# Two-layer encoder on one core: operand sums of the output product made one by one, additions to the rows by accumulating transfers, the last gate's addition two groups behind its product

## The chip, the core and the metric

The kernel runs on one core of a Trainium2 chip. The metric is device time in microseconds. The core's engines work in parallel, each through its own list of instructions in order: TensorE (PE, matrix products; PEld are its weight loads), VectorE (DVE), ScalarE (ACT), GpSimd (POOL) and SyncE (SP, which only issues transfers here). They wait for one another through semaphores. A transfer (DMA) is issued from the list of SP, ACT or POOL and then runs on its own; a transfer that adds to what stands at its target is issued from POOL here.

## What is computed

The model has two layers over 512 tokens of width 1024, with 256 memory tokens. Layer 0 mixes by dilated window attention, layer 1 by grouped-query attention; both also attend to the memory. Everything is in 32-bit floats.

```python
def reference(x, mem, norm_g, mem_norm_g, w_mem_kv, mem_qn_g, mem_kn_g, w_out, w_in_a, qn_a, kn_a, w_in_b, qn_b, kn_b):
    ...
    for i in range(DEPTH):
        h = rmsnorm(x, norm_g[i])
        mem_h = rmsnorm(mem, mem_norm_g[i])
        ...
            proj = jnp.einsum('bsd,de->bse', h, w_in_a[j])
            ...
            gate = proj[..., n_qkv + MEM_W:]
            o_mix = mixer_dilated(qkv, qn_a[j], kn_a[j], ang_a)
        ...
        o_mem = memory_attention(q_mem, mem_h, w_mem_kv[i], mem_qn_g[i], mem_kn_g[i])
        y = jnp.concatenate([o_mix, o_mem], axis=-1) * jax.nn.silu(gate)
        x = x + jnp.einsum('bse,ed->bsd', y, w_out[i])
    return x
```

The change touches the last two lines of the loop in both layers: the gated `y` (512 tokens by 1536), its product with `w_out`, and the addition to `x`.

## The kernel before

**A product in three matmuls.** Each operand is split into a high part of reduced precision and a low part with the rest. `mm3` (lines 162 to 165) multiplies high by high, high by low and low by high. Weights arrive as 128x1024 tiles `wl`; ACT casts the high part `wh` (line 285), DVE subtracts it for the low part `wo` (line 295). Of a tile of `y` the same pair is made by `put` (line 762 on ACT, 763 on DVE).

**Seven products for eight.** `s_chunk` multiplies a 2x2 grid of blocks with seven block products instead of eight, out of sums of blocks (Winograd's form). The products are called 12, 11, S1, S2, S4, S3 and 22, after the sums that go in. Each goes into a bank of PSUM (`pj`, four banks in rotation; a product marked fresh takes a new one, another adds to the bank of an earlier one). When a bank is complete, `keep` copies it to a tile `sn` (ACT, line 360) or `add` adds it to such a tile (DVE, line 370), which gives a block of the result that goes to `ev`; a `keep` also makes one difference (DVE, line 364). Until that copy or addition has read the bank, the product that takes the bank next can't start.

**The order is written out.** The program is traced once and each engine runs its instructions in the order of the trace. A `Driver` counts groups of matmuls ("slots"): `s_chunk` calls `tick` after each weight tile, and work that has been handed over with `release` (drains of banks, with a delay in slots), `spawn` (urgent) or `later` (bulk) is traced when its slot comes. A `yield n` in such work means: go on n slots later. So where an instruction stands in DVE's or ACT's list is decided by these delays.

**The output projection.** `gates` makes the gated `y` in three chunks of 512 columns: m (the memory heads), a and b (the mixer's two halves). Chunks m and a are held as `yf`, and `prep_y` (lines 751 to 795) makes from them the left operands of the seven products: 12 and 11 as they are; then, in `ys` and in place, S1 = a21 - a22, S2 = S1 - a11, S4 = a12 + S2 and S3 = a11 - a21, and last 22. Chunk b's blocks (tanh, lines 725 to 743) make `y` for a plain product in `out_rest`. `out_proj` (lines 797 to 815) loads the rows that are added to (`acc`, line 804: x, or layer 0's result), runs the seven products with 512-column tiles, whose `ev` adds each block `t` to `acc` (line 812, DVE), and then `out_rest` (line 696), which adds the product of chunk b and gives each block of rows on: to the norm of the next layer, or to the output.

In time the pieces overlap. Chunk b of the gates is still being drained when the products 12 and 11 run. In layer 0 the last head's softmax scaling (`p`, line 1097), its transposition (`pt`, line 1110) and its product also fall into the seven products, and behind them the norm of the memory rows of layer 1 (POOL, lines 412, 413 and 453). In layer 1 the attention heads run all through them, four blocks of 128 queries for each head: scores, `nmb` (the row maximum, line 1314), exponentials, `rdb` and `pb` (lines 1323, 1324), a transposition on PE, and `pbT`, whose high part ACT casts (line 1337) and whose low part DVE subtracts (line 1342), before PE multiplies by the values into `ob`.

Names in the profile: `sn` is a drained block, `th` a tanh, `og` the attention's output read back from memory (`od`, `odb`), `yS` a sum's pair of parts, `y` either the pair of 12, 11 and 22 or that of chunk b.

Of the kernel before, what the change touches and what calls it, by code (L numbers as in the profile page):

```python
# [13 lines left out]
ALU = mybir.AluOpType  # L14
# [110 lines left out]
def trunk_kernel(ctx: ExitStack, tc: tile.TileContext, x, mem, wall, norm_g, mem_norm_g, gcol,  # L125
                 qn_a, kn_a, qn_b, kn_b, ident_d, mask_d, tab_a, tab_b, out):
    nc = tc.nc
    V, A, G, T = nc.vector, nc.scalar, nc.gpsimd, nc.tensor
# [14 lines left out]
    def s2(dt=F32, name="s2"):  # L143
        return pool.tile([128, 512], dt, tag="s2", name=name, bufs=NS2)
# [204 lines left out]

    PRODUCTS = (("12", 0, True), ("11", 1, True), ("S1", 0, True), ("S2", 1, False), ("S4", 0, False), ("S3", 1, False), ("22", 0, True))  # L350

    def s_chunk(n, act, ev, tokens=True, pre=None, half=False):


        units, per = n // 256, 1024 // n
        bank, snap = [None, None], {}

        def keep(name, u, b):
            t = snap[name, u] = s2(name="sn")
            A.copy(t, b)  # L360
            yield 1
            if name == "s3":
                c = snap["s5", u]
                V.tensor_tensor(c, c, t, ALU.subtract)  # L364
                yield 1
                yield from ev("22", u, c)

        def add(q, name, u, b):
            t = snap[name, u]
            V.tensor_tensor(t, b, t, ALU.subtract if q == "12" else ALU.add)  # L370
            yield 1
            yield from ev(q, u, t)

        after = ((keep, "z"), (add, "11", "z"), (keep, "s5"), (keep, "s2"), (add, "12", "s2"), (keep, "s3"), (add, "21", "s3"))
        for i, (a, s, fresh) in enumerate(PRODUCTS):
            while a not in act:
                drv.tick()
            if fresh:
                bank[s] = [pj() for _ in range(units)]
            for x in range(units):  # L380
                wh, wo = [t.rearrange("p (k c) -> p k c", c=n) for t in W.take()]
                ah, al = act[a][:, 0], act[a][:, 1]
                for b in range(2):
                    if pre and i == x == 0 and b:
                        pre()
                    if half and b:
                        n_half[0] += 1
                        if n_half[0] % half == 0:
                            drv.half()
                    o = bank[s][b] if units == 2 else bank[s][0][:, b * 256:(b + 1) * 256]  # L390
                    bs = slice(b * 128, (b + 1) * 128)
                    for k in range(per):
                        kk = x * per + k
                        st, sp = fresh and kk == 0 and (units == 2 or b == 0), kk == 3
                        if tokens:
                            mm3(o, ah[:, kk, bs], al[:, kk, bs], wh[:, k], wo[:, k], st, sp)
                        else:
                            mm3(o, wh[:, k, bs], wo[:, k, bs], ah[:, kk], al[:, kk], st, sp)
                drv.free()
                W.advance()  # L400
                if x == units - 1:
                    f, *arg = after[i]
                    for u in range(units):
                        d = 2 if f is keep else 2 + u + (units == 1 and i == 6)
                        drv.release(f(*arg, u, bank[s][u]), d)
                drv.tick()

# [15 lines left out]
    half = pool.tile([128, 8], F32, name="half")  # L423
# [280 lines left out]
    def gates(od, o_done):  # L704

        ys, yf, y_done, YW = [None] * 4, [None, None], set(), {}

        def gate(H, first, g, half=False):


            yt = [[m4(F32R, "y").rearrange("p (h t) -> p h t", h=2) for _ in range(2)] for _ in range(2)] if g == 2 else None
            if g < 2:
                yf[g] = [m4(name="yf") for _ in range(2)]

            def ev(q, u, t):
# [12 lines left out]
                yield 1  # L728
                if not o:
                    while not {h0, h0 + 1} <= o_done:  # L730
                        yield 1
                    o = load()
                    yield 1
                if g < 2:
                    V.tensor_tensor(yf[g][j][:, i * 512:(i + 1) * 512], t, o, ALU.mult)
                    y_done.add((g, i, j))
                    return
                V.tensor_tensor(t, t, o, ALU.mult)
                yield 1
                tv = t.rearrange("p (h t) -> p h t", h=2)  # L740
                A.copy(yt[j][0][:, :, ts], tv)
                yield 1
                V.tensor_tensor(yt[j][1][:, :, ts], tv, yt[j][0][:, :, ts].bitcast(F32), ALU.subtract)
                y_done.add((g, i, j))
                if {(2, 0, j), (2, 1, j)} <= y_done:
                    for k in range(2):
                        ys[2 * j + k] = (yt[j][0][:, k], yt[j][1][:, k])

            s_chunk(256, H, ev, tokens=False, half=half)

        def prep_y():

            def wait(*gi):
                while not {(g, i, j) for g, i in gi for j in range(2)} <= y_done:
                    yield 1

            def put(k, src):
                t = big(F32R, "y" + k)
                for j in range(2):
                    js = slice(j * 512, (j + 1) * 512)  # L760
                    lo = t[:, 1024 + j * 512:1024 + (j + 1) * 512]
                    A.copy(t[:, js], src[j])
                    V.tensor_tensor(lo, src[j], t[:, js].bitcast(F32), ALU.subtract)  # L763
# [12 lines left out]
            s1 = [s2(name="ys") for _ in range(2)]  # L776
            s2_ = [s2(name="ys") for _ in range(2)]
            for j in range(2):
                V.tensor_tensor(s1[j], a21[j], a22[j], ALU.subtract)
            for j in range(2):  # L780
                V.tensor_tensor(s2_[j], s1[j], a11[j], ALU.subtract)
            yield 1
            put("S1", s1)
            yield 1
            put("S2", s2_)
            for j in range(2):
                V.tensor_tensor(a12[j], a12[j], s2_[j], ALU.add)
            for j in range(2):
                V.tensor_tensor(a21[j], a11[j], a21[j], ALU.subtract)
            yield 1  # L790
            for k, src in (("S4", a12), ("S3", a21), ("22", a22)):
                put(k, src)
                yield 1

        return gate, prep_y, YW, ys

    def out_proj(YW, ys, src, evac, tiles, half=False):

        acc, done = {}, set()

        def load():
            for i in range(2):
                for u, t in enumerate(tiles()):
                    nc.sync.dma_start(t, src[2 * i + u])
                    acc[2 * i + u] = halves(t)
                yield 2

        def ev(q, u, t):
            b, n = 2 * (int(q[0]) - 1) + u, int(q[1]) - 1
            while b not in acc:  # L810
                yield 1
            V.tensor_tensor(acc[b][n], t, acc[b][n], ALU.add)
# [26 lines left out]
    H, H2 = {}, {}  # L839
# [321 lines left out]
    gate, prep_y, YW, ys = gates(od, o_done)  # L1161
# [217 lines left out]
    gate, prep_y, YW, ys = gates(od_b, o_done_b)  # L1379
# [121 lines left out]
```

## Time and profile before

| | us |
|---|---|
| median of 3 runs | 982.19 (982.18 to 983.54) |
| the profiled execution, whole | 981.91 |
| its span, first to last instruction | 980.1 |
| DVE adding to `acc` at line 812, 16 times | 683 ns each |
| DVE idle, 580 to 600 and 900 to 920 | 1.19 and 0.11 |
| DVE idle, 600 to 620 and 920 to 940 | 3.53 and 1.99 |

The page lists each engine's busy time and share of the span. A row of PE's waits says which PE instruction waited for which instruction of another engine, for how long in total, how often, and the longest. A row of a timeline has the start, the duration, the engine, the line, the operation and the tiles (out <- in), and in brackets how long the engine sat idle ahead of it and what ended that. On DVE durations overlap a little with the next start, so the cost of an operation in a row of them is the distance of two starts. A row of the windows gives the length, then busy time (and count) of PE, PEld, DVE, ACT and POOL, the clock granted to TensorE, the share of the DMA engines and GB/s. The output projection of layer 0 lies at about 575 to 650 us, that of layer 1 at about 910 to 980.

### The profile page before, as it was taken

What the parts mean: (1) busy time and instruction counts of PE and PEld (TensorE: products, weight loads), DVE (VectorE), ACT (ScalarE), POOL (GpSimd) and SP (SyncE); (2) the same over time, 40 slices, a digit from 0 to 9 for tenths busy, and PEclk for the clock granted to TensorE, in tenths of its full rate; (3) what the DMA queues carried; (4) which work ended last, traced back from release to release, by engine and by line L of the source; (5) the groups of instructions that cost most, each with busy time, mean ns of one, the idle gap of its engine ahead of it and who ended that gap; (6) DMA issues with size and microseconds to landing.
All of it is one profiled execution on the core that took longest, in us unless ns stands there. A gap on an engine that the chain in (4) does not pass through costs nothing.

```text
span 980.1 us, 16658 instructions
## 1 busy us (share of the span) xinstructions
PE 953.1 (97%) x5728; PEld 839.5 (86%) x5728; DVE 825.1 (84%) x1489; ACT 645.7 (66%) x1623; POOL 332.2 (34%) x468
## 2 busy tenths in 40 slices
PE   8899999999999999999999989998999999998998
PEld 5789888888888888888899977887999999997786
DVE  6997788878888888888888998968789998889974
ACT  5556678686767676768676656455677766667650
POOL 1121424556555555555544010124533331011000
PEclk9999999999999999999999999999999999999999
DMA  8979846969686868686949795669695786786432
GB/s 328 329 267 322 227 97 183 290 129 266 152 253 154 251 157 248 158 249 136 271 124 295 228 251 158 258 224 329 168 209 140 189 220 165 230 207 148 144 129 86
DMA packets 86678, 205.08 MB, mean 209 GB/s; under 512 B 25025, under 2 KB 35777, under 8 KB 86594
## 3 DMA queue, kind: packets, MB, share of 16 engines
q1 hardware_dynamic: 70034, 146.28, 42.7%
q0 software_dynamic: 15264, 55.58, 30.1%
q10 hardware_dynamic: 1296, 2.16, 0.6%
q8 instruction: 45, 0.74, 0.3%
q14 instruction: 39, 0.32, 0.1%
HBM read 157.79 MB, written 12.65 MB: 174 GB/s over the span
## 4 chain that ended last, share of the span: by engine, by line
PE 75%; DVE 16%; DMA 3%; issue 2%; ACT 2%; POOL 1%; SPq 0%; DVEq 0%; POOLq 0%
PE pj L163 20%; PE pj L165 19%; PE pj L164 19%; DVE wo L295 4%; PE qT L534 2%; PE oo L1131 1%; PE sa L1029 1%; PE pt L1110 1%; PE sa L1025 1%; PE xT L464 1%; DMA od<-o 1%; DVE sn L370 1%; PE ptb L1333 1%; DVE nmb L1314 1%; DVE yS L763 1%
## 5 line engine op out<-in xcount | busy, mean ns | idle before, releaser
L295 DVE TENSOR_TENSOR wo<-wl,wh 128x1024 fp32r<-128x1024 f32 x255 | 315.5, 1242 | 8.4 <-ACT wh L285 8.0
L285 ACT CAST wh<-wl 128x1024 fp32r<-128x1024 f32 x255 | 269.9, 1059 | 74.1 <-PE pj L165 39.8
L163 PE MATMUL pj<-wh,hS 128*128 128x512 f32 (+1 forms) x448 | 164.3, 367 | 0.2 <-ACT sn L360 0.2
L164 PE MATMUL pj<-wo,hS 128*128 128x512 f32 (+1 forms) x448 | 158.1, 353 | 2.6 <-DVE wo L295 2.6
L165 PE MATMUL pj<-wh,hS 128*128 128x512 f32 (+1 forms) x448 | 158.1, 353 | 0.0
L163 PE MATMUL pj<-wh,h 128*128 128x512 f32 (+1 forms) x336 | 123.2, 367 | 0.0
L164 PE MATMUL pj<-wo,h 128*128 128x512 f32 (+1 forms) x336 | 118.8, 353 | 1.9 <-DVE wo L295 1.9
L165 PE MATMUL pj<-wh,h 128*128 128x512 f32 (+1 forms) x336 | 118.9, 354 | 0.0
L413 POOL TENSOR_TENSOR rstd<-mse,half 128x4 f32<-128x4 f32 (+2 forms) x98 | 103.4, 1055 | 8.2
L164 PEld LDWEIGHTS pj<-wo,hS 128*128 128x128 f32 x448 | 85.0, 190 | 13.4 <-DVE wo L295 3.5
L165 PEld LDWEIGHTS pj<-wh,hS 128*128 128x128 f32 x448 | 84.7, 189 | 12.4 <-DVE hS L160 0.3
L163 PEld LDWEIGHTS pj<-wh,hS 128*128 128x128 f32 x448 | 84.8, 189 | 10.3 <-ACT sn L360 0.4
L360 ACT COPY sn<-pj 128x512 f32<-128x512 f32 x132 | 73.6, 591 | 17.5 <-PE pj L165 17.1
L412 POOL TENSOR_SCALAR mse<-hss 128x4 f32<-128x4 f32 (+1 forms) x86 | 45.7, 532 | 110.2 <-ACT junk L522 103.2
L522 ACT ACTIVATE junk<-sn 128x128 f32<-128x128 f32 x264 | 79.0, 308 | 0.2 <-DVE sn L364 0.2
L973 POOL TENSOR_TENSOR ta<-sn,tabs 128x128 f32<-128x128 f32 (+1 forms) x64 | 37.0, 580 | 120.7 <-DVE sn L527 81.6
L164 PEld LDWEIGHTS pj<-wo,h 128*128 128x128 f32 x336 | 64.0, 191 | 9.5 <-DVE wo L295 2.2
L165 PEld LDWEIGHTS pj<-wh,h 128*128 128x128 f32 x336 | 63.7, 190 | 9.2 <-DVE h L160 0.2
L370 DVE TENSOR_TENSOR sn<-pj,sn 128x512 f32<-128x512 f32 x99 | 67.5, 683 | 4.6 <-PE pj L165 4.4
L163 PEld LDWEIGHTS pj<-wh,h 128*128 128x128 f32 x336 | 63.9, 190 | 7.3 <-ACT h L157 0.2
L269 POOL DMA_DIRECT2D wl<-wl x33 | 29.3, 887 | 114.5 <-DVE wo L295 70.1
L163 PE MATMUL pj<-hS,wh 128*128 128x256 f32 x192 | 55.9, 291 | 0.0
(229 smaller groups left out, 2455.7 us busy)
## 6 DMA issues: line engine op xcount, KB each, us to landing
wl<-in_wall_dram SPq DMA_DIRECT2D x222, 512.0 KB, 6.9
wl<-wl POOLq DMA_DIRECT2D x64, 512.0 KB, 5.8
wl<-in_wall_dram POOLq DMA_DIRECT2D x42, 512.0 KB, 8.3
od<-o SPq DMA_DIRECT2D x12, 256.0 KB, 5.2
og<-od SPq DMA_DIRECT2D x12, 256.0 KB, 5.9
odb<-o SPq DMA_DIRECT2D x12, 256.0 KB, 3.5
og<-odb SPq DMA_DIRECT2D x12, 256.0 KB, 4.6
x<-in_x_dram SPq DMA_DIRECT2D x4, 512.0 KB, 5.7
```

The costliest lines, as they stand in the source:

```text
L163: T.matmul(o, lh, rh, start=start, stop=False, skip_group_check=True)
L164: T.matmul(o, lh, rl, start=False, stop=False, skip_group_check=True)
L165: T.matmul(o, ll, rh, start=False, stop=stop, skip_group_check=True)
L269: G.dma_start(self.tile[key], self.tile[c, "T2", x], accum_op=ALU.add)
L285: A.copy(wh, self.tile[self.items[i]])
L295: V.tensor_tensor(wo, self.tile[key], wh.bitcast(F32), ALU.subtract)
L360: A.copy(t, b)
L370: V.tensor_tensor(t, b, t, ALU.subtract if q == "12" else ALU.add)
L412: G.tensor_scalar(e, ss, EPS, None, ALU.add)
L413: G.tensor_tensor(r, e, half[:, 0:n], ALU.pow)
L522: A.activation(jk, p[:, j * 128:(j + 1) * 128], AF.Square, scale=QS, accum_out=ss[:, j:j + 1])
L973: G.tensor_tensor(ta[:, 0:n], xn[:, 0:n, 0:32], ropeA[:, 0, b, s0:s0 + n], ALU.mult)
```

## The change

Three edits, in both layers.

First, `s_chunk` gets a parameter `soon`, true for chunk b of the gates: the addition behind its last product ("22"), which was traced three slots after it, is traced two slots after it. The difference that this addition needs (`c - t` of the kept products) is made by a helper `diff`, either in `keep` as before or ahead of the addition, whichever is traced first.

Second, `prep_y` makes a sum, then its two parts, then the next sum. S2 is made in place in S1's tiles, and the tiles `s2_` are gone. S4, S3 and 22 follow with a slot or two between each. Before, S1 and S2 were made together, and S4 and S3 together right behind the parts of S2.

Third, in `out_proj` a block is no longer added to `acc` by DVE. POOL issues a transfer that adds the block to `acc` in place, and `ev` goes on two slots later.

```diff
@@ -349,7 +349,7 @@
 
     PRODUCTS = (("12", 0, True), ("11", 1, True), ("S1", 0, True), ("S2", 1, False), ("S4", 0, False), ("S3", 1, False), ("22", 0, True))
 
-    def s_chunk(n, act, ev, tokens=True, pre=None, half=False):
+    def s_chunk(n, act, ev, tokens=True, pre=None, half=False, soon=False):
 
 
         units, per = n // 256, 1024 // n
@@ -360,13 +360,20 @@
             A.copy(t, b)
             yield 1
             if name == "s3":
-                c = snap["s5", u]
-                V.tensor_tensor(c, c, t, ALU.subtract)
+                diff(u)
                 yield 1
-                yield from ev("22", u, c)
+                yield from ev("22", u, snap["s5", u])
+
+        def diff(u):
+
+            if (u, "22") not in snap:
+                c = snap[u, "22"] = snap["s5", u]
+                V.tensor_tensor(c, c, snap["s3", u], ALU.subtract)
 
         def add(q, name, u, b):
             t = snap[name, u]
+            if name == "s3":
+                diff(u)
             V.tensor_tensor(t, b, t, ALU.subtract if q == "12" else ALU.add)
             yield 1
             yield from ev(q, u, t)
@@ -401,7 +408,7 @@
                 if x == units - 1:
                     f, *arg = after[i]
                     for u in range(units):
-                        d = 2 if f is keep else 2 + u + (units == 1 and i == 6)
+                        d = 2 if f is keep else 2 + u + (units == 1 and i == 6 and not soon)
                         drv.release(f(*arg, u, bank[s][u]), d)
                 drv.tick()
 
@@ -746,7 +753,7 @@
                     for k in range(2):
                         ys[2 * j + k] = (yt[j][0][:, k], yt[j][1][:, k])
 
-            s_chunk(256, H, ev, tokens=False, half=half)
+            s_chunk(256, H, ev, tokens=False, half=half, soon=g == 2)
 
         def prep_y():
 
@@ -774,23 +781,27 @@
             yield 1
             yield from wait((0, 1), (1, 1))
             s1 = [s2(name="ys") for _ in range(2)]
-            s2_ = [s2(name="ys") for _ in range(2)]
             for j in range(2):
                 V.tensor_tensor(s1[j], a21[j], a22[j], ALU.subtract)
+            yield 1
+            put("S1", s1)
+            yield 1
             for j in range(2):
-                V.tensor_tensor(s2_[j], s1[j], a11[j], ALU.subtract)
-            yield 1
-            put("S1", s1)
-            yield 1
-            put("S2", s2_)
+                V.tensor_tensor(s1[j], s1[j], a11[j], ALU.subtract)
+            yield 1
+            put("S2", s1)
+            yield 2
             for j in range(2):
-                V.tensor_tensor(a12[j], a12[j], s2_[j], ALU.add)
+                V.tensor_tensor(a12[j], a12[j], s1[j], ALU.add)
+            yield 1
+            put("S4", a12)
+            yield 1
             for j in range(2):
                 V.tensor_tensor(a21[j], a11[j], a21[j], ALU.subtract)
             yield 1
-            for k, src in (("S4", a12), ("S3", a21), ("22", a22)):
-                put(k, src)
-                yield 1
+            put("S3", a21)
+            yield 2
+            put("22", a22)
 
         return gate, prep_y, YW, ys
 
@@ -809,7 +820,8 @@
             b, n = 2 * (int(q[0]) - 1) + u, int(q[1]) - 1
             while b not in acc:
                 yield 1
-            V.tensor_tensor(acc[b][n], t, acc[b][n], ALU.add)
+            G.dma_start(acc[b][n], t, accum_op=ALU.add)
+            yield 2
             done.add((n, b))
 
         drv.spawn(load(), ACC_AT)
```

Lines below the first edit stand up to 15 lines lower in the changed program: DVE's addition 370 is 377 there, the difference 364 is 371, the parts of `put` 762 and 763 are 769 and 770, the sums 779, 781, 787 and 789 are 785 (S1), 790 (S2), 795 (S4) and 800 (S3), the gate's lines 727, 738 and 743 are 734, 745 and 750, and the addition 812 is the transfer 823.

DVE's list in layer 0 from the sums on, before (line, operation, out <- in, tile; x2 is two of a kind in a row). The product "11" of the output projection needs the bank that line 370 reads:

```order
L779 TENSOR_TENSOR ys<-yf 128x512 x2
L781 TENSOR_TENSOR ys<-ys,yf 128x512 x2
L738 TENSOR_TENSOR sn<-sn,og 128x512
L295 TENSOR_TENSOR wo<-wl,wh 128x1024
L763 TENSOR_TENSOR yS_7133<-ys,yS_7133 128x512 x2
L295 TENSOR_TENSOR wo<-wl,wh 128x1024
L763 TENSOR_TENSOR yS_7165<-ys,yS_7165 128x512 x2
L787 TENSOR_TENSOR yf<-yf,ys 128x512 x2
L789 TENSOR_TENSOR yf<-yf 128x512 x2
L743 TENSOR_TENSOR y<-sn,y 128x2x256
L727 SCALAR_TENSOR_TENSOR sn<-th,sn 128x512
```

Directly behind these rows, up to the gate's addition, before:

```order
L364 TENSOR_TENSOR sn<-sn 128x512
L1072 TENSOR_TENSOR nmM<-stp,oth 128x8
L1074 TENSOR_TENSOR d<-nmM,stp 128x8
L1075 TENSOR_TENSOR d<-nmM,oth 128x8
L370 TENSOR_TENSOR sn<-pj,sn 128x512
```

And the same place now, from the first sum to the gate's low part:

```order
L785 TENSOR_TENSOR ys<-yf 128x512 x2
L745 TENSOR_TENSOR sn<-sn,og 128x512
L295 TENSOR_TENSOR wo<-wl,wh 128x1024
L770 TENSOR_TENSOR yS_7129<-ys,yS_7129 128x512 x2
L371 TENSOR_TENSOR sn<-sn 128x512
L377 TENSOR_TENSOR sn<-pj,sn 128x512
L295 TENSOR_TENSOR wo<-wl,wh 128x1024
L790 TENSOR_TENSOR ys<-ys,yf 128x512 x2
L750 TENSOR_TENSOR y<-sn,y 128x2x256
```

The gate's addition (370, now 377) stood 15 rows behind the first sums, and stands five behind them now; the second sum is made behind it, and S4 and S3 (795 and 800) further on, outside these rows.

DVE's list in layer 1, where chunk b is drained among the heads, before: from one addition of a bank to the next low part of `pbT`.

```order
L370 TENSOR_TENSOR sn<-pj,sn 128x512
L295 TENSOR_TENSOR wo<-wl,wh 128x1024
L763 TENSOR_TENSOR yS_11192<-ys,yS_11192 128x512 x2
L787 TENSOR_TENSOR yf<-yf,ys 128x512 x2
L789 TENSOR_TENSOR yf<-yf 128x512 x2
L1323 RECIPROCAL rdb<-denb 128x1
L1324 TENSOR_SCALAR pb<-pb,rdb 128x512
L1314 TENSOR_REDUCE nmb<-sb 128x1
L1342 TENSOR_TENSOR pbT<-ptb,pbT 128x4x128
```

And now the rows that end at the same `pbT`, from the one ahead of it:

```order
L1354 TENSOR_TENSOR pbT<-ptb,pbT 128x4x128
L295 TENSOR_TENSOR wo<-wl,wh 128x1024
L790 TENSOR_TENSOR ys<-ys,yf 128x512 x2
L1335 RECIPROCAL rdb<-denb 128x1
L1336 TENSOR_SCALAR pb<-pb,rdb 128x512
L1326 TENSOR_REDUCE nmb<-sb 128x1
L1354 TENSOR_TENSOR pbT<-ptb,pbT 128x4x128
```

The sums S4 and S3 (787 and 789) and one operand's low parts (763) are no longer ahead of that `pbT`; S2's sum (790) is.

POOL's list in layer 0, now, from the last weight sums to the norm of the memory rows (lines 460, 419 and 420, before 453, 412 and 413):

```order
L269 DMA wl<-wl 128x1024 x2
L264 DMA wl<-in_wall_dram 128x1024 x2
L823 DMA acc<-sn 128x512 x6
L460 TENSOR_TENSOR mse<-ss 128x1
L419 TENSOR_SCALAR mse<-mse 128x1
L420 TENSOR_TENSOR rstd<-mse,half 128x1
L460 TENSOR_TENSOR mse<-ss 128x1
L419 TENSOR_SCALAR mse<-mse 128x1
L420 TENSOR_TENSOR rstd<-mse,half 128x1
L823 DMA acc<-sn 128x512 x2
L460 TENSOR_TENSOR mse<-ss 128x1
```

The eight transfers of the layer are new; the first six stand between the last weight loads and the memory rows' norm, the other two behind the first two rows' `rstd`. In layer 1 the eight stand together, with nothing behind them.

More of the change, by code (lines that the diff above doesn't have):

```diff
@@ L776, in prep_y @@
             s1 = [s2(name="ys") for _ in range(2)]
-            s2_ = [s2(name="ys") for _ in range(2)]
             for j in range(2):
                 V.tensor_tensor(s1[j], a21[j], a22[j], ALU.subtract)
-            for j in range(2):
-                V.tensor_tensor(s2_[j], s1[j], a11[j], ALU.subtract)
             yield 1
@@ L784, in prep_y @@
             yield 1
-            put("S2", s2_)
             for j in range(2):
-                V.tensor_tensor(a12[j], a12[j], s2_[j], ALU.add)
+                V.tensor_tensor(s1[j], s1[j], a11[j], ALU.subtract)
+            yield 1
+            put("S2", s1)
+            yield 2
+            for j in range(2):
+                V.tensor_tensor(a12[j], a12[j], s1[j], ALU.add)
+            yield 1
+            put("S4", a12)
+            yield 1
             for j in range(2):
```

## The prediction

> **What bounds the kernel now.** I read the page's busy times first, then PE's waits, then both output projections by windows, then the two engines' timelines there.
>
> ```profile
> span 980.1 us, 16658 instructions
> PE 953.1 (97%) x5728; PEld 839.5 (86%) x5728; DVE 825.1 (84%) x1489; ACT 645.7 (66%) x1623; POOL 332.2 (34%) x468
> ```
>
> TensorE is busy for 953.1 of 980.1 us, and the change takes no matmul away. All that it can win lies in PE's 27 us of idle time and in what follows an idle stretch. PE's waits (who waits on whom: us in total, times, longest) hold these rows on the two output projections:
>
> ```profile
> PE pj L164 <- DVE wo L295: 4.9, 5, 1.9
> PE ob L164 <- DVE pbT L1342: 4.6, 3, 2.2
> PE pj L163 <- DVE sn L370: 4.0, 1, 4.0
> PE pj L165 <- DVE y L743: 0.9, 1, 0.9
> ```
>
> Every one names VectorE. The windows (length, then busy us and count of PE, PEld, DVE, ACT, POOL, then clock, DMA share, GB/s) say why:
>
> ```profile
> 100.00:540.00 440.00, 440.00 (x2454) 380.43 (x2453) 365.99 (x780) 319.54 (x937) 225.37 (x335) 1.00 0.76 202
> 580.00:600.00 20.00, 15.59 (x64) 12.04 (x63) 18.81 (x37) 10.83 (x18) 1.75 (x2) 0.91 1.03 310
> 600.00:620.00 20.00, 19.15 (x101) 16.09 (x101) 16.47 (x23) 11.18 (x16) 0.00 (x0) 1.00 0.26 86
> 900.00:920.00 20.00, 17.77 (x97) 14.84 (x96) 19.89 (x34) 14.58 (x29) 1.76 (x2) 1.00 0.71 193
> 920.00:940.00 20.00, 19.43 (x105) 16.34 (x104) 18.01 (x31) 13.39 (x25) 0.00 (x0) 1.00 0.37 141
> ```
>
> From 100 to 540 us PE never stops. At 580 to 600 and 900 to 920 DVE is full (18.81 and 19.89 of 20) and PE isn't (15.59, 17.77): in these two stretches VectorE, and the order of its work, sets the pace. POOL does almost nothing there.
>
> **Layer 0, the late addition.** PE's timeline (start, us, instruction, idle before it):
>
> ```profile
> 581.16 0.39 PE L164 MATMUL pj<-wo,y 128*128 128x512 f32 x1
> 581.39 0.39 PE L165 MATMUL pj<-wh,y 128*128 128x512 f32 x1
> 585.75 0.50 PE L163 MATMUL pj<-wh,y 128*128 128x512 f32 x1 [3.97 <-DVE sn L370]
> 586.80 0.61 PE L164 MATMUL pj<-wo,y 128*128 128x512 f32 x1
> 590.19 0.41 PE L163 MATMUL pj<-wh,y 128*128 128x512 f32 x1
> 602.79 0.96 PE L1110 MATMUL pt<-ident,p 128*128 128x128 f32 x7 [0.45 <-DVE p L1097]
> ```
>
> The second half of "11" wants the PSUM bank that the gate's last product still holds. Matmuls follow every 0.23 us (581.16, 581.39), so it could start at 581.62 and starts at 585.75: 4.13 lost. From 586.80 to 590.19 eight matmuls take 3.39 us where eight at 0.23 take 1.84: 1.55 more, with the clock at 0.91 in that window. So the stall and its aftermath cost 5.7 us. DVE in that time:
>
> ```profile
> 572.34 1.28 DVE L779 TENSOR_TENSOR ys<-yf 128x512 f32<-128x512 f32 x2
> 573.95 1.29 DVE L781 TENSOR_TENSOR ys<-ys,yf 128x512 f32<-128x512 f32 x2 [0.33 <-DMA od<-o]
> 575.16 0.68 DVE L738 TENSOR_TENSOR sn<-sn,og 128x512 f32<-128x512 f32 x1
> 575.76 1.22 DVE L295 TENSOR_TENSOR wo<-wl,wh 128x1024 fp32r<-128x1024 f32 x1
> 576.90 1.29 DVE L763 TENSOR_TENSOR yS<-ys,yS 128x512 fp32r<-128x512 f32 x2
> ...
> 585.01 0.68 DVE L370 TENSOR_TENSOR sn<-pj,sn 128x512 f32<-128x512 f32 x1
> ...
> 590.30 1.29 DVE L763 TENSOR_TENSOR yS<-yf,yS 128x512 fp32r<-128x512 f32 x2 [1.04 <-ACT yS L762]
> ...
> 601.58 1.06 DVE L1097 TENSOR_SCALAR p<-p,c 128x192 f32<-128x192 f32 x4
> ```
>
> Prices by spacing of starts: a 128x512 operation 0.60 (575.16 to 575.76), so a pair 1.21; a `wo` 1.14 (575.76 to 576.90). In the new order the addition stands behind the S1 sums (to about 573.5), one product with the gate (574.1), one `wo` (ACT's cast permitting, about 575.5), S1's low parts (576.7) and the difference (577.3): it ends near 578.0. The bank is needed at 581.62, so there are 3.6 us of cover; a `wo` or two late would not bring the stall back. The 3.97 goes, and with it what followed.
>
> PE can't keep all 5.7. The next thing that it waits for is the second scaling of p (601.58, done 602.64), and DVE has to get there. Ahead of it, before and after, stand seven `wo`, but the low parts of three operands instead of five: two pairs fewer, 2.4 us. The removed accumulation (0.60) is made up by one more y subtraction. DVE's idle 0.33 and 1.04 in this stretch may go (the first waited for a buffer that the in-place S2 no longer takes), or come back as waits for ACT. So p is scaled 2.4 to 3.8 us earlier. I walked the new order row by row at these prices, with ACT's casts between, and it comes to 599.4 and 600.2 for PE's transposition, whose last seven run to 603.50 now: 3.3 us, my value. PE meanwhile loses some 0.9 again on a `wo`. The two delayed pairs (S3, 22) then fall where PE leads:
>
> ```profile
> 612.59 0.69 DVE L1143 TENSOR_TENSOR o<-oo,o 128x512 f32<-128x512 f32 x1 [2.94 <-PE oo L165]
> ```
>
> DVE idles 3.5 us in 600 to 620 and waits 2.94 of it here, so 2.4 are hidden. Without that cover they would cost up to 2.4. Layer 0: **3.3**, ends 0.9 (3.3 less 2.4) and 5.7.
>
> **Layer 1, the same moves among the heads.** DVE and PE, one after the other:
>
> ```profile
> 903.84 1.28 DVE L787 TENSOR_TENSOR yf<-yf,ys 128x512 f32<-128x512 f32 x2
> 905.04 1.28 DVE L789 TENSOR_TENSOR yf<-yf 128x512 f32<-128x512 f32 x2
> 907.43 0.68 DVE L1342 TENSOR_TENSOR pbT<-ptb,pbT 128x512 fp32r<-128x512 f32 x1
> 952.22 0.68 DVE L812 TENSOR_TENSOR acc<-sn,acc 128x512 f32<-128x512 f32 x1
> ```
>
> ```profile
> 908.17 0.39 PE L164 MATMUL ob<-pbT,vb 128*128 128x256 f32 x1 [2.23 <-DVE pbT L1342]
> 927.68 0.39 PE L164 MATMUL ob<-pbT,vb 128*128 128x256 f32 x1 [0.57 <-DVE pbT L1342]
> 955.90 0.50 PE L165 MATMUL pj<-wh,y 128*128 128x512 f32 x1 [0.92 <-DVE y L743]
> ```
>
> Since the pbT three heads' steps earlier, DVE does two pairs of sums and one pair of low parts less in the new order (S2 goes behind, S4 and S3 further still): 3 x 1.2 = 3.6 us. The pbT at 907.43 comes at about 903.8; PE wants it at 908.17 - 2.23 = 905.94: the 2.23 goes. Up to the pbT behind the 0.57, one accumulation more is gone, 4.2 us in all, against a PE that runs 2.3 earlier: the 0.57 goes. Then S4, S3 and 22 come, and DVE's lead over PE falls to some 0.3 to 1.2 us by my walk; DVE's 2 us of idle time in 920 to 940 is the cover. Of the 0.92 one accumulation (952.22, 0.60) stood directly ahead: 0.3 stays. Sum 2.23 + 0.57 + 0.6 = **3.4**; ends 1.0 (lead lost at two or three pbT, about 0.8 each) and 3.7. The stall of 1.8 at 885 lies ahead of all this and stays. The last 20 us are paced by PE on both sides.
>
> **The accumulating transfers.** They take 16 additions from DVE and put 16 transfers on POOL's queue:
>
> ```profile
> L812 DVE TENSOR_TENSOR acc<-sn,acc x16: 678/683/685, 601.0 to 961.6; 128x512 f32<-128x512 f32 x16
> L269 POOL DMA_DIRECT2D wl<-wl x33: 850/876/950, 31.0 to 892.0; - x33
> DMA to landing us min/median/max: 4.4/5.0/9.7
> 629.15 2.76 POOL L413 TENSOR_TENSOR rstd<-mse,half 128x1 f32<-128x1 f32 x1
> ```
>
> The nearest row is L269, a transfer on chip that adds 512 KB to its target: 0.88 us of POOL, landing 4.4 to 9.7 us after issue, median 5.0. Ours are half as large; I take 5.0. POOL: 16 x 0.88 = 14 us, free by the windows. In layer 0 six of eight are queued ahead of the memory rows' norm; the other two stand behind its first `rstd` (629.15, 2.76 us) and land near 637, where the remaining rows' additions want them at about 637 to 640. POOL's later `wl` sums, queued behind them, have some 12 us in hand by my walk, so only an evacuation off PE's path could wait. Price 0, at most 2. In layer 1 the tile `sn` that a transfer reads isn't free until it lands, and ACT's copy of a later product takes that buffer. By the walk the transfer is issued at 920.2 and the copy is due at 923.5; behind it on ACT stand the cast of the next weights and the high part of a pbT that PE wants around 928. So landing up to 5 or 6 us costs nothing, and each us beyond costs one; at the 9.7 of the row it costs 4.
>
> SP's queue gets no new instruction. But in layer 0 its loads of the rows to be added to (`acc`) wait for buffers that the y sums hold until their low parts are made, and S4, S3 and 22 are now made later; the weight loads behind them on SP follow some us later. No row above has PE waiting for a weight transfer, so I price this at 0; if the loads came too late, ACT's cast, then `wo`, then PE would wait, a us for a us.
>
> One rule speaks against this. The Trainium skill, page "SBUF — State Buffer", in its trap "DVE blocks DMA", says that a DMA issued from GpSimd can't get its descriptors written while VectorE holds the shared port in its two-port mode, and it tells of one that took 3100 ns instead of 620. The L269 rows speak against its weight here, as 33 issues among a DVE that is 83% busy spread only from 850 to 950 ns; were it so all the same, the landing would by that page be some 2.5 us longer, an estimate, and 975.5 would become about 977.5. The page "DMA: Bandwidth & Descriptors", section on the anatomy of one DMA, gives 2.0 us + bytes/436e3, an estimated 2.6 us for 256 KB, below every row here.
>
> **Sum.** 3.3 + 3.4 - 0 = 6.7. The profiled execution took 981.91 us for its 980.1 us span, so 1.81 lies around the span and stays: 981.91 - 6.7 = 975.2. The median of the runs is 0.28 above that execution: **975.5 us**.
>
> **Rivals.**
>
> *A, the transfers hold ACT (slower).* The mechanism is the `sn` buffer of layer 1. For it: the landing of the rows reaches 9.7, and DMA is at 0.71 in 900 to 920. Against: 5.0 is the median. It decides from a landing of about 5.5 + 6.7 = 12.2 us if one copy is held, or 8.9 if two are. At 10.5 us and two copies held it costs 2 x 5 = 10 and gives 982.2 - 6.7 + 10 = 985.5.
>
> *B, the stalls only move.* DVE has the same work but for 16 x 0.60, and its lead of 0.3 to 1.2 us in layer 1 is within the error of my walk. Layer 0 at 0.9 and layer 1 at 1.0 to 2.0: 982.2 - 2.4 = 979.8. For it: DVE is full in both windows. Against: it idles 3.5 and 2.0 us in the windows right behind.
>
> *C, the whole of the first stall comes back.* If ACT's casts keep up, DVE's `wo` need not hold PE at 593 to 600; 5.7 + 3.4 = 9.1, or 973.1. For it: 1.04 of DVE's idle time there was only a wait for ACT. Against: the 2.4 to 3.8 of the count. The page "TensorE: Matmul & The Clock Gate", Part 1, says that an idle window of about 3.4 us halves the clock for the next; the rows agree (3.97 idle, then 3.39 us of slow matmuls; no slow ones behind the 2.23).
>
> *D, the change doesn't move the addition.* If the tile that the addition takes, or the difference ahead of it, is itself late, the bank stays held and only DVE's order further on changes: within 1 us of 982. Against: at 585.01 the addition starts straight behind its predecessor, with no wait of its own in the row; it is late by its place in DVE's queue alone, and that place is what moves.
>
> **How the numbers follow.** A difference under 0.2%, 2 us, can't be told from none. Forecast (974 to 977) 0.50; C 0.12; B 0.20, of which three quarters are faster than 980.2; A 0.12; D 0.06. Faster 0.50 + 0.12 + 0.15 = 0.77; same 0.05 + 0.06 = 0.11; slower 0.12. The range goes from just below C, 972.0, to 981.0 above most of B; A and most of D are left out.
>
> **What would show it.** Right: no PE wait on the `sn` addition, no clock below 1.00 around 580 to 600, PE's wait on the scaled p ending near 599.5 instead of 602.79, the 2.23 and 0.57 waits on pbT gone, the y wait at 0.3 or less, landings of the new transfers near 5 us. Wrong: PE waits on `wo` or pbT growing by what the others lost (B), ACT waiting for a DMA ahead of its copies in layer 1 (A), or a landing over 9 us.

## The result, and the profile after

The change makes no difference that can be measured.

| | us, median | runs | ratio to before, 95% |
|---|---|---|---|
| before | 982.71 (981.48 to 984.23) | 13 | |
| changed | 982.81 (980.34 to 984.93) | 13 | 0.9997 (0.9989 to 1.0005) |

The forecast was 975.5. The profiled execution of the changed kernel took 983.15 us with a span of 981.4. Its page and its PE waits, the rows that answer to those shown of before:

```profile
span 981.4 us, 16676 instructions
PE 955.3 (97%) x5728; PEld 839.9 (86%) x5728; DVE 816.7 (83%) x1473; ACT 645.5 (66%) x1623; POOL 344.1 (35%) x484
```

```profile
PE ob L164 <- DVE pbT L1354: 5.0, 3, 2.6
...
PE pt L1122 <- DVE p L1109: 2.1, 2, 1.6
...
PE ptb L1345 <- ACT y L748: 1.8, 1, 1.8
PE pj L165 <- DVE y L750: 1.3, 1, 1.3
...
PE pj L163 <- DVE sn L377: 0.4, 1, 0.4
```

DVE lost 8.4 us of work and 16 instructions, and POOL got 16 transfers, as written. The 4.0 us wait on the gate's addition is gone (the 0.4 is another, of a product). But PE waits longer for `pbT` (5.0 us in all, 4.6 before) and for `p` (2.1, 0.9 before), and there is a new row: `ptb`, the heads' transposition, waits 1.8 us for an ACT instruction of the gate.

PE runs the same 5728 matmuls in the same order in every kernel here. So the start of one matmul in a profile, less its start in the profile of before, says how far PE is ahead (minus) at that place, and a step in that number says where time is won or lost. By the place in the kernel before:

| place, us | what lies there | changed less before, us |
|---|---|---|
| 574.7 | ahead of the layer 0 projection | 0.53 |
| 590.5 | behind the removed stall | -5.34 |
| 602.0 | p's transposition | -1.94 |
| 640 | layer 0 done | -1.99 |
| 900 | layer 1, heads and gates | -0.78 |
| 917 | behind the second removed stall | -3.28 |
| 934.5 | last heads | -0.43 |
| 937 | | 0.60 |
| 975.7 | end | 1.24 |

Half a microsecond was lost in the first 30 us, where nothing is changed. Layer 0 wins 2.5 us (0.53 to -1.99), of which 1.2 is lost in 260 us that the change doesn't touch. Layer 1 wins 2.5 us by 917, and loses 2.9 by 934.5 and 1.7 more to the end. PE's rows at these places:

```profile
582.14 0.39 PE L163 MATMUL pj<-wh,y 128*128 128x512 f32 x1
...
595.02 0.50 PE L164 MATMUL pj<-wo,yS 128*128 128x512 f32 x1 [0.57 <-DVE wo L295]
596.83 0.50 PE L163 MATMUL pj<-wh,yS 128*128 128x512 f32 x1 [0.39 <-DVE sn L377]
600.09 0.30 PE L1122 MATMUL pt<-ident,p 128*128 128x128 f32 x1 [1.61 <-DVE p L1109]
...
884.83 0.39 PE L164 MATMUL ob<-pbT,vb 128*128 128x256 f32 x1 [2.56 <-DVE pbT L1354]
...
921.43 0.63 PE L1345 MATMUL ptb<-ident,pb 128*128 128x128 f32 x4 [1.83 <-ACT y L748]
...
927.26 0.39 PE L164 MATMUL ob<-pbT,vb 128*128 128x256 f32 x1 [1.66 <-DVE pbT L1354]
...
936.13 0.39 PE L164 MATMUL ob<-pbT,vb 128*128 128x256 f32 x1 [0.76 <-DVE pbT L1354]
957.18 0.50 PE L165 MATMUL pj<-wh,y 128*128 128x512 f32 x1 [1.30 <-DVE y L750]
```

At 582.14 the second half of "11" starts with no wait. What is lost at 921.43 and 927.26 is explained on DVE. Two of its rows before:

```profile
920.43 0.68 DVE L738 TENSOR_TENSOR sn<-sn,og 128x512 f32<-128x512 f32 x1
...
924.55 0.68 DVE L738 TENSOR_TENSOR sn<-sn,og 128x512 f32<-128x512 f32 x1
```

And now:

```profile
915.68 0.68 DVE L745 TENSOR_TENSOR sn<-sn,og 128x512 f32<-128x512 f32 x1
920.00 0.69 DVE L745 TENSOR_TENSOR sn<-sn,og 128x512 f32<-128x512 f32 x1 [3.63 <-DMA og<-odb]
...
921.80 0.68 DVE L1354 TENSOR_TENSOR pbT<-ptb,pbT 128x512 fp32r<-128x512 f32 x1
```

Two blocks of gate b are multiplied with `og`, the heads' output read back from memory. Before, the two multiplications stood one slot apart, and neither waited. Now they stand side by side, because the addition that makes the second block comes a slot earlier, and the second waits 3.63 us for its `og`. Everything behind it on DVE waits too: the heads' scaling, `nmb` and `pbT`. PE's transposition at 921.43 reads the heads' scaled block, which DVE finishes at 921.28; the row names ACT's cast of the gate's block (L748), which waits for the same multiplication and ends at 921.34. The `pbT` that PE waits 1.66 us for starts on DVE at 926.52, and from 920.00 to there DVE is never idle. SP's queue shows what the second read stands behind:

```profile
908.50 0.33 SPq L1236 DMA_DIRECT2D odb<-o  x1
912.25 0.38 SPq L727 DMA_DIRECT2D og<-odb  x1
912.68 0.96 SPq L815 DMA_DIRECT2D acc<-x1d  x2
913.69 0.43 SPq L727 DMA_DIRECT2D og<-odb  x1
914.17 0.99 SPq L815 DMA_DIRECT2D acc<-x1d  x2
```

Two loads of 512 KB go out ahead of it and two right behind it. It is issued at 913.69 and DVE goes on at 920.00, 6.3 us later. Before, the same read stood among the same loads, issued at 914.92, but DVE came for it only 9.6 us later, at 924.55.

### The profile page after: what moved, and what is told of

It is laid out like the page before. It is cut to its first block, busy times and chain, and to the rows that moved or that the text cites. A ratio compares the mean times of both kernels' runs of the same rounds, so it can differ in the third digit from the quotient of the medians.

```text
span 981.4 us, 16676 instructions
## 1 busy us (share of the span) xinstructions
PE 955.3 (97%) x5728; PEld 839.9 (86%) x5728; DVE 816.7 (83%) x1473; ACT 645.5 (66%) x1623; POOL 344.1 (35%) x484
## 4 chain that ended last, share of the span: by engine, by line
PE 77%; DVE 12%; DMA 6%; ACT 2%; issue 2%; POOL 1%; SPq 0%; DVEq 0%; ACTq 0%; POOLq 0%
PE pj L163 20%; PE pj L165 20%; PE pj L164 20%; DVE wo L295 3%; PE qT L541 2%; DMA og<-od 2%; DMA odb<-o 2%; PE sa L1041 1%; PE oo L1143 1%; PE pt L1122 1%; PE sa L1037 1%; PE xT L471 1%; PE ptb L1345 1%; DMA og<-odb 1%; POOL tabs L1223 1%
## 5 line engine op out<-in xcount | busy, mean ns | idle before, releaser
L420 POOL TENSOR_TENSOR rstd<-mse,half 128x4 f32<-128x4 f32 (+2 forms) x98 | 98.4, 1005 | 8.2
L269 POOL DMA_DIRECT2D wl<-wl x33 | 29.3, 888 | 111.2 <-DVE wo L295 61.0
```

The source lines that it names most:

```text
L269: G.dma_start(self.tile[key], self.tile[c, "T2", x], accum_op=ALU.add)
L420: G.tensor_tensor(r, e, half[:, 0:n], ALU.pow)
```

## The experiments

The comparisons are with runs of the kernel before on the same chip, made beside them (32, 23 and 11 runs, medians 982.54, 982.55 and 982.12).

| kernel | us, median (runs) | ratio to before, 95% |
|---|---|---|
| earlier addition alone | 984.68 (12) | 1.0024 (1.0010 to 1.0038) |
| sums one by one alone | 978.71 (9) | 0.9966 (0.9951 to 0.9981) |
| transfers alone | 982.06 (12) | 0.9995 (0.9983 to 1.0007) |
| sums and transfers | 977.41 (6) | 0.9944 (0.9929 to 0.9958) |
| addition and sums | 983.18 (12) | 1.0004 (0.9992 to 1.0016) |
| the change, addition earlier in layer 0 only | 979.98 (12) | 0.9966 (0.9955 to 0.9977) |
| the change, `acc` loaded earlier in layer 1 | 978.59 (12) | 0.9964 (0.9950 to 0.9978) |
| the change, second `og` multiplication a slot later | 978.71 (6) | 0.9956 (0.9942 to 0.9970) |
| sums and transfers, last six additions on DVE | 975.08 (5) | 0.9935 (0.9922 to 0.9947) |
| sums and transfers, S3 a slot later in layer 0 | 975.63 (6) | 0.9941 (0.9921 to 0.9960) |
| both of the last two | 974.46 (4) | 0.9923 (0.9910 to 0.9936) |

**The addition earlier in layer 0 only.**

```diff
-            s_chunk(256, H, ev, tokens=False, half=half, soon=g == 2)
+            s_chunk(256, H, ev, tokens=False, half=half, soon=g == 2 and H is not H2)
```

> The changed kernel, but the last gate's addition is two groups behind its product in layer 0 only. Theory (read-back): in layer 1 the earlier addition puts both multiplications with og into one slot, and DVE stands 3.63 us for an og that is still behind loads of acc; PE then waits 1.83, 1.66 and 0.76. Here the second multiplication is a slot later again: DVE's wait on og near 918 falls under 0.5, PE's offset to the kernel before no longer rises by 3.9 between 918 and 936, and the time is 978.5 to 979.8 where the change has 982.8. Rival (transfers): the accumulating transfers cost layer 1 its gain; they are all still here, so PE's waits stay and the time is 982 to 983. Rival (order of the sums): S4, S3 and 22 made later use up DVE's lead; PE still waits 2 or more on pbT between 918 and 936, time 981 to 982.

979.98, just above what was expected, and by its ratio 979.2. The wait on `og` near 918 is gone, and between 900 and 934.5 PE wins 3.3 us (-0.22 to -3.55) where the change wins 2.5 and loses 2.9. The transfers are all there, so they are not the cause of that loss.

**The loads of `acc` earlier in layer 1.**

```diff
-        drv.spawn(load(), ACC_AT)
+        drv.spawn(load(), at)
...
-    out_proj(YW, ys, x1d, ev_o2, acc_b, HALF.get("o"))
+    out_proj(YW, ys, x1d, ev_o2, acc_b, HALF.get("o"), at=1)
```

> The changed kernel, but the loads of acc in layer 1 are issued three slots earlier on SP, so no 512 KB load stands between or ahead of the two og reads; the additions and transfers are as in the change. Theory (read-back): both og reads land within 3.5 us of their issue, DVE's wait on og near 916 to 920 falls from 3.63 to under 1, and the time is 978.5 to 980. If the slot alone is to blame and not what the read queues behind, the wait stays above 2.5 and the time at 982 or more. Rival (transfers): unchanged, 982 to 983, or better by less than 1 as the first transfer no longer waits for its rows.

978.59. Nothing of the order on DVE was touched, only what stands beside the reads on SP. The two reads, issued at 910.83 and 911.30, land 2.7 and 2.9 us later, and DVE no longer waits for them. So it takes both for the loss: the multiplication a slot earlier, and a read that is issued among four large loads.

**The second `og` multiplication a slot later, all else as changed.**

```diff
                 V.scalar_tensor_tensor(t, th, 1.0, t, ALU.add, ALU.mult)
...
+                if q == "21" and H is H2:
+                    yield 1
                 V.tensor_tensor(t, t, o, ALU.mult)
```

> The changed kernel with one thing undone: in layer 1 the second multiplication with og waits one slot more; the additions, the sums, the transfers and all loads stay as changed. Theory (read-back): DVE's 3.63 us wait on og near 918 is gone (under 0.3), PE's waits of 1.83 and 1.66 with it, PE's offset to the kernel before stays below -2 from 918 to 936; 978.5 to 980. Rival (transfers, or the queue on SP itself): no change, 982 or more.

978.71. The first line of this diff is context. DVE's two rows, now a slot apart and without a wait, and PE's next waits:

```profile
913.20 0.68 DVE L747 TENSOR_TENSOR sn<-sn,og 128x512 f32<-128x512 f32 x1
...
918.52 0.68 DVE L747 TENSOR_TENSOR sn<-sn,og 128x512 f32<-128x512 f32 x1
```

```profile
929.91 0.39 PE L164 MATMUL ob<-pbT,vb 128*128 128x256 f32 x1 [0.74 <-DVE pbT L1356]
949.76 0.50 PE L164 MATMUL pj<-wo,y 128*128 128x512 f32 x1 [0.60 <-DVE wo L295]
951.56 0.50 PE L165 MATMUL pj<-wh,y 128*128 128x512 f32 x1 [1.30 <-DVE y L752]
```

PE's waits of 1.83 and 1.66 are gone. The 0.74 and the 1.30 are still there: they have other causes.

**The three edits alone, and two pairs.** The edits are those of the change, one or two at a time.

> The kernel before with the earlier addition alone; sums and accumulation as before. Theory: the 3.97 us PE wait on the addition in layer 0 goes, but DVE has the same work ahead of the second scaling of p, so PE arrives there at most 1.4 us earlier (DVE's idle 0.33 and 1.04); in layer 1 the 2.23 wait on pbT stays, as the sums still stand ahead of it. Time 980.8 to 982.5. Rival: the whole of the 4 to 5.7 us comes back with the addition alone, 977 to 978.5. Rival: the joined og multiplications cost as in the change even here, over 984.

984.68, slower than expected, and for none of the reasons given. In layer 0 the stall on the addition goes, and PE stops again some 1.7 us of work later, on `wo`:

```profile
586.94 0.50 PE L164 MATMUL pj<-wo,y 128*128 128x512 f32 x1 [3.27 <-DVE wo L295]
595.97 0.50 PE L164 MATMUL pj<-wo,yS 128*128 128x512 f32 x1 [1.70 <-DVE wo L295]
```

DVE's rows say why: between two low parts of the weights stand S2's low parts, S4, S3 and two operations of the gate.

```profile
579.37 1.22 DVE L295 TENSOR_TENSOR wo<-wl,wh 128x1024 fp32r<-128x1024 f32 x1
580.50 1.29 DVE L770 TENSOR_TENSOR yS<-ys,yS 128x512 fp32r<-128x512 f32 x2
581.70 1.29 DVE L794 TENSOR_TENSOR yf<-yf,ys 128x512 f32<-128x512 f32 x2
582.91 1.29 DVE L796 TENSOR_TENSOR yf<-yf 128x512 f32<-128x512 f32 x2
...
585.67 1.22 DVE L295 TENSOR_TENSOR wo<-wl,wh 128x1024 fp32r<-128x1024 f32 x1
```

The next `wo` is 6.3 us behind the last one. The place that the addition left is filled by the same work, and the next thing that this work delays is the next weight tile. PE loses 1.5 us over layer 0 by this (0.27 at 574.7, 1.75 at 640).

In layer 1 it loses 2.4 more between 900 and 912 (-0.64 to 1.78): the wait on `pbT` at 908 grows from 2.23 to 3.12, and the matmuls behind it are slow. The joined multiplications with `og` are not the reason: DVE waits 1.49 us there, and PE moves by 0.3 at most.

> The kernel before with the sums made one by one alone. Theory: the sums carry most of the gain in both layers. Layer 0: the addition ends about 581.6, PE's wait on it falls from 3.97 under 1, p is scaled 2 to 2.5 us earlier. Layer 1: the 2.23 wait on pbT goes, the og multiplications stay one slot apart and don't wait; with DVE's 16 additions still there some wait on pbT of up to 1 stays near 927 to 936. Time 978 to 980. Rival (order of the sums uses up DVE's lead): PE waits 2 or more between 918 and 936, time 981 to 983.

978.71, as expected. Of the three edits only this one is faster by itself. PE's last two waits in layer 1 are here:

```profile
932.57 0.39 PE L164 MATMUL ob<-pbT,vb 128*128 128x256 f32 x1 [1.34 <-DVE pbT L1346]
953.11 0.50 PE L165 MATMUL pj<-wh,y 128*128 128x512 f32 x1 [1.08 <-DVE y L743]
```

> The kernel before with the accumulating transfers alone. Theory: nothing of the stalls that bound it goes: 3.97 on the addition and 2.23 on pbT stay, the 0.57 goes, the last y wait grows from 0.92 to about 1.3 by the slower odb store (4.1 against 2.04 us). Time within 1 us of before, 981.7 to 983. Rival (transfers hold ACT or slow the loads): 984 or more.

982.06: its interval includes no change. Both large stalls stay:

```profile
585.70 0.60 PE L163 MATMUL pj<-wh,y 128*128 128x512 f32 x1 [3.56 <-DVE sn L370]
...
907.82 0.39 PE L164 MATMUL ob<-pbT,vb 128*128 128x256 f32 x1 [2.20 <-DVE pbT L1343]
```

By the starts of its matmuls the transfers win 0.6 us by 927.68, where the 0.57 wait is gone, and lose 1.0 again by 955.90, at the last wait on `y`.

> The kernel before with the sums one by one and the accumulating transfers, without the earlier addition. If the transfers gain what they take off DVE, this is faster than the sums alone (978.7) by 0.5 to 1. My theory: they gain nothing. The 0.74 to 1.34 wait on pbT near 933 falls to about 0.75, but the last store of odb lands 4.1 to 4.2 us after its issue instead of 2.05, as in all runs with transfers so far, and PE's last wait on y goes from 1.08 to 1.3. Time 978 to 979.5. If the transfers harm more than that, 980 or more.

977.41, a little faster than expected, and better than the sums alone by the medians; but the two ratios, 0.9944 (0.9929 to 0.9958) and 0.9966 (0.9951 to 0.9981), overlap, so whether the transfers bring anything beside the sums is open.

> The changed kernel with DVE's additions to acc in place of the transfers. Theory (read-back): the wait on og stays, 3 to 4 us on DVE, and DVE now has one or two additions of 0.60 more ahead of the next pbT: PE waits 1.5 to 2.5 twice between 918 and 930, and the time is 981.5 to 983.5, no better than the change; the last odb store lands in 2.05 and the y wait is about 1. Rival (transfers are the cost in layer 1): 978 to 979.5.

983.18. The wait on `og` is there without any transfer:

```profile
921.51 0.69 DVE L745 TENSOR_TENSOR sn<-sn,og 128x512 f32<-128x512 f32 x1 [3.21 <-DMA og<-odb]
```

Taken together: the sums one by one win 0.34%, and adding the earlier addition to them takes that away, with the transfers or without. In layer 0 alone the addition isn't shown to gain either: with it there, sums and transfers are at 0.9966, and without it at 0.9944.

**Toward a better version.** The last six additions of layer 1 on DVE again:

```diff
-            G.dma_start(acc[b][n], t, accum_op=ALU.add)
-            yield 2
+            if move is None or q in move:
+                G.dma_start(acc[b][n], t, accum_op=ALU.add)
+                yield 2
+            else:
+                V.tensor_tensor(acc[b][n], t, acc[b][n], ALU.add)
...
-    out_proj(YW, ys, x1d, ev_o2, acc_b, HALF.get("o"))
+    out_proj(YW, ys, x1d, ev_o2, acc_b, HALF.get("o"), move=("11",))
```

> The sums one by one with the transfers (as in the run of both, 977.4), but the last six additions of layer 1 are on DVE again, so that no accumulating transfer is in flight when the last block of odb is stored. If the transfers slow that store, it lands in about 2.05 us again instead of 4.14, and PE's last wait on y falls from 1.30 to 1.1 or less; time 976.8 to 977.8. If the store is slow for another reason (the weight load beside it, the time of day in the kernel), it stays above 3.5.

975.08, faster than expected. The store landed 2.05 us after its issue, as expected, but PE's wait on `y` is 1.20, not 1.1 or less. Two things take the gain back. The `og` reads behind the store now took 3.7 and 3.8 us instead of 2.6 and 2.8, so that DVE has `og` only 0.7 us earlier, measured against the time at which PE wants `y`. And the addition that is on DVE again stands between `og` and `y` and costs 0.6.

S3 a slot later in layer 0 (`late` is true there):

```diff
             put("S4", a12)
-            yield 1
+            yield 2 if late else 1
             for j in range(2):
                 V.tensor_tensor(a21[j], a11[j], a21[j], ALU.subtract)
-            yield 1
+            if not late:
+                yield 1
             put("S3", a21)
```

> The sums one by one with the transfers, and in layer 0 the sum S3 (two operations, 1.2 us of DVE) is made one slot later, behind the second scaling of p. My reading of layer 0 is that DVE's work ahead of that scaling sets what comes back of the stall: then the scaling is 1.2 us earlier, PE's wait on p falls from 1.0 to 1.6 to under 0.5, PE's gain there is 0.8 to 1.2 larger, and the time is 976.3 to 977.3. If something else is late (ACT, p itself), the wait on p stays at 1 or more.

975.63, faster than expected. PE's first wait on `p`, 1.0 in the kernel that this one was made from, is gone, and the second stays:

```profile
595.97 0.50 PE L163 MATMUL pj<-wh,yS 128*128 128x512 f32 x1 [1.00 <-DVE sn L370]
598.18 0.95 PE L1116 MATMUL pt<-ident,p 128*128 128x128 f32 x7 [0.44 <-DVE p L1103]
```

So DVE's work ahead of that scaling made this wait. How much PE gains by its going is less sure: from 574.7 to 602.0 PE wins 5.1 us here, and 3.4 and 4.5 in the two profiles that have the same layer 0 but for S3, and the intervals of sums and transfers with S3 moved and not moved overlap.

> Both of these edits together, the best version that the runs point to: 975.8 to 977. If the gain of layer 0 is swallowed in layer 1 at the wait on pbT near 885 (that wait grew from 1.81 to 2.6 in most runs with an earlier layer 0), it is no better than the better of the two.

974.46, 0.77% (0.64 to 0.90) faster than before and the best version that was run. It leaves out the earlier addition altogether. It is faster than expected; that its two edits add up can't be told from these intervals.

## Why the prediction was wrong

**Layer 0, the late addition: right in its mechanism.** PE's 3.97 us wait went, PE did not keep the 5.7, and the second scaling of p was next. The term was 3.3. From 574.7 to 602.0 PE won 2.5 in the changed kernel (0.53 to -1.94), and 3.0, 3.2 and 3.1 in the three other profiles of the same order in layer 0. In part the walk was too fast: PE's wait on p ended at 600.84, not near 599.5, and DVE also waited 0.59 for an `og` read in layer 0. What the prediction did not see is that the sums do this without the earlier addition: in the three profiles that leave it out and have S3 where the change has it, PE won 3.9, 3.4 and 4.5 us over the same stretch. In two of them the wait on the gate's addition is gone, and in the third it is 1.07, where it was 3.97.

**Between the layers: not considered.** The prediction added the gains of both layers. In the changed kernel 1.2 us of layer 0's gain was gone at 900. Of it 0.75 went at 885.65, where PE's wait on `pbT` grew from 1.81 to 2.56. ACT's exponential ahead of that `pbT` waits for a buffer until a store to `odb` lands, and that store landed 7.0 us after its issue instead of 4.5. In the other profiles that stretch, 640 to 900, moved by -2.4 to +1.5 with nothing edited in it, so this is no fixed price.

**Layer 1: the failed step.** "Up to the pbT behind the 0.57, one accumulation more is gone, 4.2 us in all, against a PE that runs 2.3 earlier: the 0.57 goes." The count of DVE's work was right: the 2.23 went, and PE won 2.5 there. But the step asked only how much DVE has to do, and not whether what it does next has its operands. The prediction priced the earlier addition in layer 0 alone. In layer 1 it also moves the second multiplication with `og` a slot ahead, onto a read that takes 6.3 us beside the loads of `acc`. DVE stood for 3.63 us, the 0.57 became 1.66, and PE lost 2.9 us by 934.5, more than the 2.5 that it had won. Three kernels that undo this, in three ways, are faster than before by 0.34 to 0.44%.

**SP's queue.** "No row above has PE waiting for a weight transfer, so I price this at 0" looked at the weight loads. The transfer that mattered in that queue was the `og` read, and DVE waited for it.

**The last wait on y: wrong.** It was to fall from 0.92 to 0.3 because one accumulation stood ahead of it; it rose to 1.30, and is 0.9 to 1.3 in all profiles. DVE's rows where it gets `og`, before:

```profile
950.96 1.34 DVE L738 TENSOR_TENSOR sn<-sn,og 128x512 f32<-128x512 f32 x2 [3.36 <-DMA og<-odb]
```

And now:

```profile
952.82 1.36 DVE L745 TENSOR_TENSOR sn<-sn,og 128x512 f32<-128x512 f32 x2 [4.63 <-DMA og<-odb]
```

The 0.6 itself was won: from this row to PE's start behind the wait it took 4.94 us (950.96 to 955.90) and takes 4.36 (952.82 to 957.18). But before, DVE gets `og` 4.0 us ahead of the time at which PE wants `y`, and now only 3.1 us ahead. In the seven profiles with the late transfers (the last six of layer 1) that lead is 3.0 to 3.1, and in the six without them 3.6 to 4.1. In the seven the store ahead of the read lands about 2 us later. So the transfers took away at the read at least what they gave at the addition. The wait of DVE for `og` stood in the profile of before, and the prediction did not look at it.

**The lead over pbT.** A wait of 0.73 to 0.76 on `pbT` near 927 to 936 is in every profile that has the sums one by one with transfers, about the 0.8 for one `pbT` that the low end of the range assumed. With the sums alone it is 1.34.

**Rival A** can be ruled out for this kernel. The transfers took

```profile
L823 POOL DMA_DIRECT2D acc<-sn x16: 862/867/1195, 594.3 to 959.3; - x16
...
DMA to landing us min/median/max: 3.2/5.6/9.4
```

a median of 5.6 us where 5.0 was assumed. The longest, 9.4, is past the 9 us that the prediction named as a sign of being wrong, but ACT's copy waited for one of them for 0.35 us:

```profile
924.01 0.59 ACT L360 COPY sn<-pj 128x512 f32<-128x512 f32 x1 [0.35 <-DMA acc<-sn]
```

POOL's issues show no sign of the trap "DVE blocks DMA" of the Trainium skill's page "SBUF — State Buffer": at 867 ns median they are as short as L269's 876 before, and the longest took 1195.

**Rivals B and D.** Rival D, within 1 us of 982, comes nearest to the time, and its mechanism is wrong: the addition did move. Rival B, that the stalls only move, gave 979.8, and not by the mechanism that it named: with the `og` multiplication moved back, DVE's lead is enough for all but waits of 0.21 and 0.74 us on `pbT`.

## What to carry to other kernels

An instruction that is moved ahead in an engine's queue brings the arrival times of all its operands with it: look up when each one lands, DMA reads above all, because a single late one holds everything behind it. Test the edits of one change by themselves: here one of the three carried the gain, one took it away again, and their sum read as "no difference". Where an engine's order is the same in two kernels, subtract the starts of the same instructions; the steps in that difference name the place of each gain and loss.

## What the runs showed of the hardware

**A small store beside accumulating transfers.** The last store of 256 KB to `odb` lands 2.0 us after its issue in the profile before, and in all five other profiles without the late transfers (2.0 to 2.1). In the seven with them it takes 4.1 to 4.2. In the changed kernel one transfer was issued 2.3 and another 0.6 us ahead of it.

**The clock after a short idle.** The changed kernel and the one with the addition earlier in layer 0 only have the same instructions in the same order until layer 1's gates. In both PE waits 1.6 and 0.46 us for `p` within 2.4 us. In the windows right behind it (length, then PE, PEld, DVE, ACT, POOL, clock, DMA share, GB/s) the first had

```profile
602.00:606.00 4.00, 4.00 (x27) 3.56 (x26) 4.00 (x7) 1.42 (x2) 0.00 (x0) 1.00 0.73 262
```

and the second

```profile
602.00:606.00 4.00, 4.00 (x22) 3.40 (x22) 4.00 (x6) 0.24 (x1) 0.00 (x0) 0.82 0.68 252
```

a clock of 1.00 and of 0.82. Of the five profiles with such waits of 2.1 us in sum three show a slow stretch that costs some 1.6 us, and two none. The page "TensorE: Matmul & The Clock Gate" of the Trainium skill, Part 1, says that the clock is halved after an idle window of about 3.4 us, and that this window is free-running. The lower clock stands here behind less idle time than such a window is long, so these rows do not bear out that a whole idle window is needed. Whether the place of the window decides between the three profiles and the two is not shown by any run. Executions of one kernel spread over 1.7 us (6 runs) to 7.7 us (12 runs) here, and this may be a part of it.
